# Four other byte offsets for the normed and the gated activations of a two-layer decoder trunk

## The chip, the cores and the metric

The kernel runs on one core of one Trainium2 chip. Times are device microseconds (us) of one execution, from its first to its last instruction on that core and with what the launch adds around them. A time is read as the median over runs.

## The reference

The program is a decoder trunk of two layers over 256 tokens of width 1024, all in float32. Each layer is: a SwiGLU feed forward, a token mixer, attention to a memory of 256 rows, and a second SwiGLU feed forward, each with an RMS norm before and after it.

```python
def swiglu(x, w_gate, w_up, w_down):
    return (jax.nn.silu(x @ w_gate) * (x @ w_up)) @ w_down
...
for l in range(DEPTH):                       # DEPTH = 2
    h = swiglu(rms_norm(x, ng[0]), ffn_w_gate[l, 0], ffn_w_up[l, 0], ffn_w_down[l, 0])
    x = x + 0.5 * rms_norm(h, ng[1])
    h = mixer(rms_norm(x, ng[2]))            # RWKV-7 and retention in layer 0,
    x = x + rms_norm(h, ng[3])               # sparse latent attention and a convolution in layer 1
    h = memory_xattn(rms_norm(x, ng[4]), mem_n, xa_wq[l], xa_wk[l], xa_wv[l], xa_wo[l])
    x = x + rms_norm(h, ng[5])
    h = swiglu(rms_norm(x, ng[6]), ffn_w_gate[l, 1], ffn_w_up[l, 1], ffn_w_down[l, 1])
    x = x + 0.5 * rms_norm(h, ng[7])
```

The four feed forwards are called (0, 0), (0, 1), (1, 0) and (1, 1) below: layer, and first or second of the layer. A weight of gate or up has 1024 rows and 2816 columns, one of down 2816 rows and 1024 columns.

## The kernel before, in words

**Products in parts.** Every float32 operand of the large products is split into two fp32r tiles, a high part (`whi`, `hhi`, `ahi`; a copy on ScalarE, L198, L241 and L251) and the rest (`wlo`, `hlo`, `alo`; a subtraction on VectorE, L199, L247 and L252). One product is then three matmuls (`mm3`, L255 to L258): high by high, high by low, low by high, added up in one PSUM bank. Each matmul has its own weight load on TensorE: an operand that is loaded (128x128, the *stationary* one) and an operand that streams through it column by column (the *moving* one).

**The tiles in question.** The normed activations of a feed forward, transposed, lie in a pair `hhi`, `hlo` that `new_h` allocates (L118): 8 blocks of 256 tokens side by side, one block for each 128 features. The gated activations, transposed too, lie in pairs `ahi`, `alo` (and `ahi0`, `alo0` for the first 512 features) that `products` allocates inside `ffn` (L483). In the built program each of these tiles begins on a multiple of 256 bytes in its partition. Each is allocated 64 elements (256 bytes) longer than its data, and the data begin 48 elements, that is 192 bytes, after the tile's beginning:

```python
return tuple(p.tile([P, DT * S + 64], F32R, name=name, bufs=1)[:, shift:shift + DT * S].rearrange(
    "p (k n) -> p k n", k=DT) for name in ("hhi", "hlo"))        # shift=48
...
return tuple(fp.tile([P, n * S + 64], F32R, name=part + name, bufs=bufs)[:, 48:48 + n * S].rearrange(
    "p (k n) -> p k n", k=n) for part in ("ahi", "alo"))
```

The weight tiles `whi` and `wlo` begin on a multiple of 256 bytes without an offset. The pairs that the mixers and the attention hand to their output projections (`new_h(keep, 0)`) have offset 0. The mixers' own input pair and the memory's pair have 192.

**A feed forward** (`ffn`, L478) first makes 512 columns of gate and up with the activations stationary (128 tokens at a time) and the weights moving: matmuls of 512 columns (L429, L434 in `project`, or L256 to L258 by `proj_nat`). Then come nine groups of 256 columns (`group_t`, `proj_t`): here a 128x128 block of the weight is stationary and the activations are moving, 256 columns (the 256 tokens) in each matmul, 48 for gate (`pg`) and 48 for up (`pu`) in a group. Behind each group the down projection of the features before it follows (`down`, tile `pd`): the gated activations are stationary and the weights of down are moving, 512 columns in each matmul.

**Order.** Inside the nine groups a scheduler sets the order by data and buffers; at the seams between stages (`bridge`, `lead_in`, `mix_in`, `start`) the order is written out by hand. All weights come by SP's DMA queue as float32 into `wst` and are split on ScalarE and VectorE beside the matmuls.

Of the kernel before, what the change touches and what calls it, by code (L numbers as in the profile page):

```python
# [11 lines left out]
F32R = mybir.dt.float32r  # L12
# [5 lines left out]
P = 128  # L18
S = 256
# [75 lines left out]
def tile_hybrid_trunk(ctx: ExitStack, tc: tile.TileContext, a: dict, out: bass.AP, stop=None):  # L95
# [13 lines left out]
    def bank(tag, name):  # L109
        return psum.tile([P, 512], F32, name=name, tag=tag)  # L110
# [3 lines left out]
    pv = keep.tile([P, 56], F32, name="pv")  # L114
    hneg = keep.tile([P, 4], F32, name="hneg")
    ones = keep.tile([P, 32], F32, name="ones")[:, 0:1]

    def new_h(p, shift=48):  # L118

        return tuple(p.tile([P, DT * S + 64], F32R, name=name, bufs=1)[:, shift:shift + DT * S].rearrange(  # L120
            "p (k n) -> p k n", k=DT) for name in ("hhi", "hlo"))
# [87 lines left out]
    def wunit(w, k0, kt, c0, n, only=None):  # L209
        return unit(*wload(w, k0, kt, c0, n), only)  # L210

    def nat(w, n=512):
        return [wload(w, 2 * i, 2, 0, n) for i in range(4)]
# [36 lines left out]
    def split(src, hi, lo):  # L250
        nc.scalar.activation(hi, src, AF.Copy)  # L251
        nc.vector.tensor_sub(lo, src, f32(hi))  # L252

    def mm3(ps, lh, rh, first, last):
        (l_hi, l_lo), (r_hi, r_lo) = lh, rh  # L255
        nc.tensor.matmul(ps, l_hi, r_hi, start=first, stop=False)  # L256
        nc.tensor.matmul(ps, l_hi, r_lo, start=False, stop=False)  # L257
        nc.tensor.matmul(ps, l_lo, r_hi, start=False, stop=last)  # L258


    def proj_nat(ps, h, t, units, kt):
        k = 0
        tot = len(units) * kt
        for hi, lo in units:
            for i in range(kt):
                s = slice(t * P, (t + 1) * P)
                mm3(ps, (h[0][:, k, s], h[1][:, k, s]), (hi[:, i, :], lo[:, i, :]), k == 0, k == tot - 1)
                k += 1
# [11 lines left out]
    def group_t(w, c0, h, name, us=None):  # L280
        us = us or [wunit(w, 4 * i, 4, c0, 256) for i in range(2)]
        ps = bank("pa", name)
        for f in range(2):
            proj_t(ps[:, f * S:(f + 1) * S], h, us, 4, f)
        return ps
# [132 lines left out]
    def in_order():  # L418
        return tc.manual_schedule(engines={ET.DVE, ET.Activation, ET.PE})
# [56 lines left out]
    def ffn(l, j, h, fp, lead, gpost, nxt, mid=None, follow=None):  # L476
        wg, wu, wd = a["ffn_w_gate"][l, j], a["ffn_w_up"][l, j], a["ffn_w_down"][l, j]
        pss = None  # L478
        kt_total = FF // P
        kt_at = 0  # L480

        ug, uu, done = lead
        def products(name, n, bufs):  # L483

            return tuple(fp.tile([P, n * S + 64], F32R, name=part + name, bufs=bufs)[:, 48:48 + n * S].rearrange(
                "p (k n) -> p k n", k=n) for part in ("ahi", "alo"))

        act = products("0", 4, 1)
        for t in range(2):
            if t < len(done):  # L490
                pg, pu = done[t]
            else:
                pg, pu = bank("pa", "pg"), bank("pa", "pu")
                proj_nat(pg, h, t, ug, 2)
                proj_nat(pu, h, t, uu, 2)
            sg = fp.tile([P, 512], F32, name="sg", bufs=2)
            nc.scalar.activation(sg, pg, AF.Silu)
            nc.vector.tensor_mul(sg, sg, pu)
            tr = bank("fr", "tra")
            for i in range(4):  # L500
                nc.tensor.transpose(tr[:, i * P:(i + 1) * P], sg[:, i * P:(i + 1) * P], ident)
            o = (slice(None), slice(None), slice(t * P, (t + 1) * P))
            split(tr.rearrange("p (k n) -> p k n", k=4), act[0][o], act[1][o])

        pss = [[bank(tag, "pd") for tag in ("iv", "bk")] for _ in range(2)]

        def down_unit(kt):
            return wunit(wd, kt, 1, 0, D)

        def down(act, i, kt, t, u, qs=(0, 1)):  # L510
            s = slice(t * P, (t + 1) * P)
            for q in qs:
                c = slice(q * 512, (q + 1) * 512)
                mm3(pss[t][q], (act[0][:, i, s], act[1][:, i, s]), (u[0][:, 0, c], u[1][:, 0, c]),
                    kt == 0, kt == kt_total - 1)

        todo = [(act, i, i) for i in range(4)]
        ngroups = (FF - 512) // 256
        for g in range(ngroups):
            if g > 1 and mid:  # L520
                next(mid, None)
            if g == 1:
                gpost = gpost()
            c0 = 512 + 256 * g
            pg = group_t(wg, c0, h, "pg")
            pu = group_t(wu, c0, h, "pu")
            sg = fp.tile([P, 512], F32, name="sg", bufs=2)
            nc.scalar.activation(sg, pg, AF.Silu)
            af = fp.tile([P, 512], F32, name="af", bufs=2)
            nc.vector.tensor_mul(af, sg, pu)  # L530
            act = products("", 2, 2)
            fl = lambda z: z.rearrange("p k n -> p (k n)")
            split(af, fl(act[0]), fl(act[1]))
            if g < ngroups - 1:
                for (ac, i, kt) in todo:
                    u = down_unit(kt)
                    for t in range(2):
                        down(ac, i, kt, t, u)
                todo = []
            todo += [(act, i, 4 + 2 * g + i) for i in range(2)]  # L540
        if follow:
            gn, hn, loads, only = follow
            ahead = units_ahead([(*wload(wd, kt, 1, 0, D), only) for (_, _, kt) in todo] + loads)
            ahead.load(3)
            us = ahead.take(4)
            po = [post(pss[t], gpost, t, True) for t in range(2)]
            no = [rms(env["x"][:, t, :], gn, hn, t) for t in range(2)]

            def tp(t, q):

                order = {(0, 0): ((0, 0), (0, 1), (1, 0), (1, 1), (0, 2), (0, 3)), (0, 1): ((1, 2), (1, 3))}
                for c, i in order.get((t, q), [(q, i) for i in range(4)]):
                    down(*todo[i], t, us[i], (c,))

            with in_order():
                bridge(tp, po, no, ahead, 3 if only is None else 3)
                return nxt(po[1], no[1], hn, ahead)

        us = [down_unit(kt) for (_, _, kt) in todo]
        for t in range(2):  # L560
            for q in range(2):
                for e, u in zip(todo, us):
                    down(*e, t, u, (q,))
            post(pss[t], gpost, t, True).all()
            nxt(t)
# [38 lines left out]
    def cross(l, sp, y, w_unit, w_out, kts):  # L604
# [1 line left out]
        wq, wo = a["xa_wq"][l], a["xa_wo"][l]  # L606
        wg, wu = a["ffn_w_gate"][l, 1], a["ffn_w_up"][l, 1]
        sc = 128.0 ** -0.5
        h, h2 = new_h(sp), new_h(sp)
        cx = ExitStack()  # L610
        xp = cx.enter_context(tc.tile_pool(reuse_waits="tile", name=f"xa{l}", bufs=1))
        gp, gn = ng(l, 3), ng(l, 4)
# [33 lines left out]
        o = new_h(keep, 0)  # L646
# [953 lines left out]

    with stage("0", None, None, 4) as sp:
        env["x"] = sp.tile([P, 2, D], F32, name="x", bufs=1)
        h = new_h(sp)
        hm, _ = ffn_mix(0, sp, h, keep, start(h), early())
        mem_k(0, mh, memp)
    for l in range(depth):
        if l % 2 == 0:
            y, w_unit = even_mixer(l, hm, mh if l == 0 else None, mem_scope if l == 0 else None)
            kts = [0, 1, 2, 3, 4, 5, 6, 7]
        else:  # L1610
            y, w_unit = odd_mixer(l, hm, pss)
            hm_scope.close()
            kts = [4, 5, 6, 7, 0, 1, 2, 3]
        if l == 0:
            xpool = pool("x", side="right", reuse_waits="tile")
        with stage(f"x{l}", [xd[t] for t in range(2)] if l == 0 else None, xpool) as sp:
            h2, lead = cross(l, sp, y, w_unit, a["od_w_out" if l % 2 else "ev_w_out"][l // 2], kts)
            with tc.tile_pool(reuse_waits="tile", name=f"ffb{l}", bufs=1) as fp:
                if l + 1 < depth:
                    h3 = new_h(sp)  # L1620
                    lead = ffn(l, 1, h2, fp, lead, lambda: ng(l, 7), lead_in,
                               follow=(ng(l + 1, 0), h3, nat(a["ffn_w_gate"][l + 1, 0]) + nat(a["ffn_w_up"][l + 1, 0]), None))
                else:
                    ffn(l, 1, h2, fp, lead, lambda: ng(l, 7), finish)
            if l + 1 < depth:
                hm_scope = ExitStack()
                hm, pss = ffn_mix(l + 1, sp, h3, hm_scope.enter_context(
                    tc.tile_pool(name=f"hm{l + 1}", bufs=1, side="right", reuse_waits="tile")), lead)
# [45 lines left out]
```

## Time and profile before

| | |
|---|---|
| median of 2 runs | 1194.47 us (1193.23 to 1195.7) |
| the profiled execution's own time | 1193.1 us |
| its span in the trace | 1191.2 us |
| TensorE busy with matmuls | 1139.0 us (96%), 7956 matmuls |
| TensorE busy with weight loads | 1006.0 us (84%) |
| VectorE, ScalarE, GpSimd busy | 727.9, 608.5, 69.9 us |
| DMA, mean over the span | 180 GB/s |

A matmul's duration in the trace overlaps that of the next one, since matmuls are pipelined. What a matmul takes of the time is read from the distance between its start and the next one's start: two rows of the timeline and the number of matmuls between them give it. In the rows below, names such as `pu<-hhi,whi` read: the PSUM tile that is written, then the moving operand, then the stationary one.

### The profile page before, as it was taken

What the parts mean: (1) busy time and instruction counts of PE and PEld (TensorE: products, weight loads), DVE (VectorE), ACT (ScalarE), POOL (GpSimd) and SP (SyncE); (2) the same over time, 40 slices, a digit from 0 to 9 for tenths busy, and PEclk for the clock granted to TensorE, in tenths of its full rate; (3) what the DMA queues carried; (4) which work ended last, traced back from release to release, by engine and by line L of the source; (5) the groups of instructions that cost most, each with busy time, mean ns of one, the idle gap of its engine ahead of it and who ended that gap; (6) DMA issues with size and microseconds to landing.
All of it is one profiled execution on the core that took longest, in us unless ns stands there. A gap on an engine that the chain in (4) does not pass through costs nothing.

```text
span 1191.2 us, 19770 instructions
## 1 busy us (share of the span) xinstructions
PE 1139.0 (96%) x7956; PEld 1006.0 (84%) x7956; DVE 727.9 (61%) x1097; ACT 608.5 (51%) x908; POOL 69.9 (6%) x104
## 2 busy tenths in 40 slices
PE   6999999999998989999999999999899999999997
PEld 5899999997776767799999789999788777899996
DVE  5645555587567587755554755454669588654552
ACT  5545445754334567644443654444456467544441
POOL 0000000012241010000000000000100000000000
PEclk9999999999999999999999999999999999999999
DMA  6877665643652775476665476665433664676650
GB/s 217 247 256 227 206 182 173 195 154 102 170 158 77 217 270 157 157 220 193 199 192 176 135 237 209 196 186 166 140 89 89 224 218 124 212 214 205 188 171 36
DMA packets 152267, 213.99 MB, mean 180 GB/s; under 512 B 21872, under 2 KB 115184, under 8 KB 152176
## 3 DMA queue, kind: packets, MB, share of 16 engines
q1 hardware_dynamic: 138224, 206.58, 56.5%
q10 hardware_dynamic: 13216, 3.54, 1.3%
q0 software_dynamic: 736, 2.62, 0.7%
q8 instruction: 62, 1.02, 0.3%
q14 instruction: 29, 0.24, 0.1%
HBM read 206.67 MB, written 6.05 MB: 179 GB/s over the span
## 4 chain that ended last, share of the span: by engine, by line
PE 71%; DVE 12%; ACT 5%; DMA 5%; issue 3%; POOL 2%; ACTq 0%; SPq 0%; POOLq 0%; DVEq 0%
PE pd L258 6%; PE pd L257 6%; PE pd L256 6%; PE pg L258 6%; PE pg L257 6%; PE pg L256 6%; PE pu L257 6%; PE pu L256 6%; PE pu L258 6%; DVE wlo L199 2%; DVE wlo L247 2%; POOL rstd L304 1%; ACT whi L198 1%; PE trh L353 1%; ACT sq L326 1%
## 5 line engine op out<-in xcount | busy, mean ns | idle before, releaser
L199 DVE TENSOR_TENSOR wlo<-wst,whi 128x1024 fp32r<-128x1024 f32 x290 | 356.0, 1229 | 307.7 <-ACT whi L198 303.2
L198 ACT ACTIVATE whi<-wst 128x1024 fp32r<-128x1024 f32 x290 | 306.9, 1060 | 329.7 <-PE pg L257 66.5
L257 PE MATMUL pg<-hlo,whi 128*128 128x256 f32 x576 | 160.2, 278 | 0.0
L256 PE MATMUL pg<-hhi,whi 128*128 128x256 f32 x576 | 160.2, 278 | 0.0
L258 PE MATMUL pg<-hhi,wlo 128*128 128x256 f32 x576 | 160.0, 278 | 0.0
L258 PE MATMUL pu<-hhi,wlo 128*128 128x256 f32 x576 | 159.2, 276 | 0.0
L256 PE MATMUL pu<-hhi,whi 128*128 128x256 f32 x576 | 159.1, 276 | 0.0
L257 PE MATMUL pu<-hlo,whi 128*128 128x256 f32 x576 | 159.1, 276 | 0.0
L258 PE MATMUL pd<-whi,alo 128*128 128x512 f32 x352 | 138.6, 394 | 0.0
L257 PE MATMUL pd<-wlo,ahi 128*128 128x512 f32 x352 | 137.8, 393 | 0.0
L256 PE MATMUL pd<-whi,ahi 128*128 128x512 f32 x352 | 137.2, 390 | 0.0
L257 PEld LDWEIGHTS pg<-hlo,whi 128*128 128x128 f32 x576 | 108.9, 189 | 1.4
L256 PEld LDWEIGHTS pg<-hhi,whi 128*128 128x128 f32 x576 | 108.6, 188 | 1.4
L258 PEld LDWEIGHTS pg<-hhi,wlo 128*128 128x128 f32 x576 | 108.7, 189 | 0.0
L247 DVE TENSOR_TENSOR wlo<-wst,whi 128x1024 fp32r<-128x1024 f32 (+1 forms) x68 | 81.8, 1215 | 43.5 <-ACT whi L241 42.5
L257 PEld LDWEIGHTS pu<-hlo,whi 128*128 128x128 f32 x576 | 108.3, 188 | 0.0
L258 PEld LDWEIGHTS pu<-hhi,wlo 128*128 128x128 f32 x576 | 108.1, 188 | 0.0
L256 PEld LDWEIGHTS pu<-hhi,whi 128*128 128x128 f32 x576 | 108.1, 188 | 0.0
L241 ACT ACTIVATE whi<-wst 128x1024 fp32r<-128x1024 f32 (+1 forms) x68 | 70.3, 1052 | 36.0 <-PE pu L257 9.1
L304 POOL TENSOR_TENSOR rstd<-s,hneg 128x1 f32<-128x1 f32 x34 | 23.9, 703 | 943.9 <-DVE s L374 943.9
L258 PEld LDWEIGHTS pd<-whi,alo 128*128 128x128 f32 x352 | 66.2, 188 | 14.1 <-DVE alo L252 0.6
L256 PEld LDWEIGHTS pd<-whi,ahi 128*128 128x128 f32 x352 | 66.1, 188 | 13.8 <-ACT ahi L251 0.7
(374 smaller groups left out, 2010.5 us busy)
## 6 DMA issues: line engine op xcount, KB each, us to landing
wst<-in_ffn_w_gate_dram SPq DMA_DIRECT2D x88, 512.0 KB, 4.5
wst<-in_ffn_w_up_dram SPq DMA_DIRECT2D x88, 512.0 KB, 4.3
wst<-in_ffn_w_down_dram SPq DMA_DIRECT2D x88, 512.0 KB, 4.4
wst<-in_ev_w_in_dram SPq DMA_DIRECT2D x30, 512.0 KB, 3.9
gb<-in_norm_g_dram SPq DMA_DIRECT2D x16, 512.0 KB, 5.9
wst<-in_od_w_in_dram SPq DMA_DIRECT2D x12, 512.0 KB, 4.2
wst<-in_xa_wk_dram SPq DMA_DIRECT2D x8, 512.0 KB, 4.4
wst<-in_xa_wv_dram SPq DMA_DIRECT2D x8, 512.0 KB, 4.3
```

Of the source, the lines that this page charges most:

```text
L198: nc.scalar.activation(hi[:, :m], st[:, :m], AF.Copy)
L199: env["split"] = nc.vector.tensor_sub(lo[:, :m], st[:, :m], f32(hi[:, :m])).ins
L241: nc.scalar.activation(hi[:, :kt * n], st[:, :kt * n], AF.Copy)
L247: env["split"] = nc.vector.tensor_sub(lo[:, :m], st[:, :m], f32(hi[:, :m])).ins
L256: nc.tensor.matmul(ps, l_hi, r_hi, start=first, stop=False)
L257: nc.tensor.matmul(ps, l_hi, r_lo, start=False, stop=False)
L258: nc.tensor.matmul(ps, l_lo, r_hi, start=False, stop=last)
L304: nc.gpsimd.tensor_tensor(dst, src, hneg[:, :n], op=ALU.pow)
L326: nc.scalar.activation(sq, self.src[:, q * 512:(q + 1) * 512], AF.Square, scale=1.0 / math.sqrt(D), accum_out=self.ss[:, q:q + 1])
L353: nc.tensor.transpose(tr[:, i * P:(i + 1) * P], self.xg[q][:, i * P:(i + 1) * P], ident)
```

## The change

Nothing but byte offsets changes. A table gives each feed forward its own offset, in elements of 4 bytes: 52, 44, 56 and 40, which is 208, 176, 224 and 160 bytes, for (0, 0), (0, 1), (1, 0) and (1, 1). `products` takes it for the gated activations, and the four calls of `new_h` that make a feed forward's normed activations take it too. All tiles keep their places and their sizes; on each of the five engines the same instructions stand in the same order, with the same waits. In one feed forward these operands move: the moving operand of 864 matmuls of 256 columns (9 groups of 96), the stationary operand of 96 matmuls of 512 columns for gate and up and of 264 for down, and the places that ScalarE and VectorE write (15 splits each). In four feed forwards that makes 3456, 384 and 1056 matmuls. The mixers, the memory's keys and values, and the attention's output projection keep their offsets.

```diff
+    OFF_LINES = {(0, 0): 52, (0, 1): 44, (1, 0): 56, (1, 1): 40}
...
         def products(name, n, bufs):
 
-            return tuple(fp.tile([P, n * S + 64], F32R, name=part + name, bufs=bufs)[:, 48:48 + n * S].rearrange(
+            o = OFF_LINES[l, j]
+            return tuple(fp.tile([P, n * S + 64], F32R, name=part + name, bufs=bufs)[:, o:o + n * S].rearrange(
                 "p (k n) -> p k n", k=n) for part in ("ahi", "alo"))
...
-        h, h2 = new_h(sp), new_h(sp)
+        h, h2 = new_h(sp), new_h(sp, OFF_LINES[l, 1])
...
-        h = new_h(sp)
+        h = new_h(sp, OFF_LINES[0, 0])
...
-                    h3 = new_h(sp)
+                    h3 = new_h(sp, OFF_LINES[l + 1, 0])
```

## Rows read from the trace of the kernel before

**Rows 1.** The page: span, busy time, granted clock by slice, chain by engine.
```profile
span 1191.2 us, 19770 instructions
...
PE 1139.0 (96%) x7956; PEld 1006.0 (84%) x7956; DVE 727.9 (61%) x1097; ACT 608.5 (51%) x908; POOL 69.9 (6%) x104
...
PEclk9999999999999999999999999999999999999999
...
PE 71%; DVE 12%; ACT 5%; DMA 5%; issue 3%; POOL 2%; ACTq 0%; SPq 0%; POOLq 0%; DVEq 0%
```

**Rows 2.** Windows: the four feed forwards' groups; window: length, busy by engine, clock, DMA.
```profile
42.60:203.00 160.40, 160.40 (x1137) 149.13 (x1137) 89.85 (x94) 79.54 (x101) 2.03 (x3) 1.00 0.70 215
502.30:662.00 159.70, 159.02 (x1132) 148.03 (x1132) 84.31 (x84) 73.04 (x85) 1.16 (x2) 1.00 0.64 191
688.70:851.00 162.30, 160.32 (x1133) 148.40 (x1132) 84.75 (x87) 74.48 (x87) 1.48 (x2) 1.00 0.63 189
1024.30:1184.00 159.70, 159.08 (x1132) 147.75 (x1131) 79.86 (x79) 67.67 (x77) 0.55 (x1) 1.00 0.57 175
```

**Rows 3.** Costliest groups by form: line, tiles, shapes, count | busy us, mean ns.
```profile
L257 PE MATMUL pg<-hlo,whi 128*128 128x256 f32 x576 | 160.2, 278 | 0.0
...
L258 PE MATMUL pd<-whi,alo 128*128 128x512 f32 x352 | 138.6, 394 | 0.0
...
L429 PE MATMUL pg<-whi,hhi 128*128 128x512 f32 x40 | 16.5, 413 | 0.5 <-ACT hhi L251 0.5
...
L256 PE MATMUL pu<-whi,hhi 128*128 128x512 f32 x24 | 9.3, 388 | 0.0
```

**Rows 4.** Timeline of TensorE, second group of (0, 0): start us, duration us, instruction.
```profile
70.48 0.28 PE L256 MATMUL pu<-hhi,whi 128*128 128x256 f32 x1
...
75.92 0.39 PE L256 MATMUL pd<-whi,ahi 128*128 128x512 f32 x1
```

**Rows 5.** Timeline of TensorE, first group of (0, 0).
```profile
48.17 0.28 PE L256 MATMUL pu<-hhi,whi 128*128 128x256 f32 x1
...
53.82 0.40 PE L256 MATMUL pd<-whi,ahi 128*128 128x512 f32 x1
```

**Rows 6.** Timeline of TensorE at half clock, before that group.
```profile
42.78 0.41 PE L256 MATMUL pg<-hhi,whi 128*128 128x256 f32 x1
...
43.42 0.41 PE L256 MATMUL pg<-hhi,whi 128*128 128x256 f32 x1
```

**Rows 7.** Timeline of TensorE behind down projections, and an output projection's two ends.
```profile
65.02 0.28 PE L256 MATMUL pg<-hhi,whi 128*128 128x256 f32 x1
65.14 0.29 PE L257 MATMUL pg<-hlo,whi 128*128 128x256 f32 x1
65.27 0.28 PE L258 MATMUL pg<-hhi,wlo 128*128 128x256 f32 x1
65.39 0.28 PE L256 MATMUL pg<-hhi,whi 128*128 128x256 f32 x1
...
81.42 0.28 PE L256 MATMUL pg<-hhi,whi 128*128 128x256 f32 x1
...
936.90 0.39 PE L256 MATMUL po<-whi,hhi 128*128 128x512 f32 x1
...
947.78 0.39 PE L256 MATMUL po<-whi,hhi 128*128 128x512 f32 x1
```

**Rows 8.** Timeline of TensorE in the mixer of layer 1, matmuls of 456 columns.
```profile
852.76 0.37 PE L429 MATMUL pdi<-wlo,hhi 128*128 128x456 f32 x1
852.97 0.37 PE L429 MATMUL pdi<-whi,hhi 128*128 128x456 f32 x1
...
856.68 0.99 PE L434 MATMUL pdi<-whi,hlo 128*128 128x456 f32 x4
```

**Rows 9.** Splits on L252 and L251 by tile: ns min/median/max, first and last start.
```profile
L252 DVE TENSOR_TENSOR alo<-af,ahi x36: 683/686/693, 55.8 to 1175.0; 128x512 fp32r<-128x512 f32 x36
...
L252 DVE TENSOR_TENSOR hlo<-yc,hhi x2: 685/686/686, 933.9 to 939.6; 128x512 fp32r<-128x512 f32 x2
...
L251 ACT ACTIVATE ahi<-af x36: 614/632/636, 54.7 to 1174.3; 128x512 fp32r<-128x512 f32 x36
...
L251 ACT ACTIVATE hhi<-yc x2: 633/634/635, 932.9 to 938.6; 128x512 fp32r<-128x512 f32 x2
```

## The prediction, made before the changed kernel had run

> **What bounds the kernel now.** I read the page first. TensorE is busy with matmuls for 1139.0 of 1191.2 us, the clock is granted in full in all 40 slices, and the chain that ends last runs over TensorE for 71% [rows 1]. Then the windows of the four feed forwards: in each, matmuls fill all but 2 us of some 160 us, while VectorE and ScalarE are busy for about half of it and the DMA engines for 0.57 to 0.70 [rows 2]. So the distance between the starts of two matmuls is the price of everything here, and the change touches just the operands of these matmuls: 3456 of 256 columns (two products of three matmuls, 576 each), 1056 of 512 columns for down (three of 352) and 384 of 512 columns for gate and up (six groups of 40, six of 24) [rows 3].
>
> The timeline gives the distances. The reader is to see that one and the same form has two levels. In the second group of (0, 0), 48 matmuls of 256 columns take 75.92 - 70.48 = 5.44 us, 113.3 ns each [rows 4]. In the first group 48 of the same form, on the same activations with the same 192 bytes, take 53.82 - 48.17 = 5.65 us, 117.7 ns each [rows 5]. For 512 columns: from 53.82 to 65.02 there are 48 for down, 233.3 ns each [rows 5, 7]; from 75.92 to 81.42 there are 24, 229.2 ns each [rows 4, 7]; and in the output projection, where the stationary operand lies on a 256-byte line, 48 from 936.90 to 947.78 take 226.7 ns each [rows 7]. The switch is seen at 65.02: the first three distances of the next group are 0.12, 0.13 and 0.12 us, and from 65.39 to 70.48 the other 45 take 113.1 ns each [rows 7, 4]. Order, waits and clock are alike on both sides, so the level is a matter of how the reads of the moving operand and of the next weight load fall against each other. An offset can change that.
>
> At half clock (1.2 GHz) the same matmul took (43.42 - 42.78) / 3 = 213 ns [rows 6]; half of that is 106.7 ns for 256 columns at 2.4 GHz. The lower level is 6.6 ns above it, so at full clock something beside the columns is paid for, in proportion to the bytes: 226.7 for 512 columns is twice 113.3 [rows 4, 7]. Cut into 64-byte stretches (16 columns), 256 columns are 16 of them, 7.08 ns each, of which 6.67 are the columns and 0.41 is the rest. 192 bytes are three such stretches; none of 208, 176, 224 and 160 is a whole number of them, so 1024 bytes of data touch 17 stretches where they touched 16. That is the whole change for a moving operand.
>
> **The change part by part.**
>
> *Instructions.* None is added, removed or moved, on no engine and in no DMA queue, so no wait changes its place: 0 us.
>
> *Moving operand, 3456 matmuls.* The price of the 17th stretch has no row of its own. Its lower bound is the 0.41 ns for one more edge: 3456 x 0.41 = 1.4 us. Its upper bound is a whole stretch although only part of it is used: 3456 x 7.08 = 24.5 us. The nearest row is the mixer's projection, whose moving operand has 456 columns (28.5 stretches) and begins on a 256-byte line in one matmul and 32 bytes after one in the next. Touched are 29 stretches either way. Whole stretches would make 29 x 7.08 = 205.4 ns, used bytes 28.5 x 7.08 = 201.9 ns; 19 matmuls from 852.76 to 856.68 took 206.3 ns each [rows 8]. What the 512-column matmuls with a stationary operand at 192 bytes pay over 226.7 ns is 2.5 ns at the lower level and 6.6 ns at the upper. By used bytes the mixer pays 4.4 ns, between these two; by whole stretches 0.9 ns, below both. The row is nearer to used bytes, and I take +1.4 us. An offset of 32 bytes is not paid twice over in any case, which speaks for 224 and 160; for 208 and 176, which are 16 bytes off, no row speaks.
>
> [...]
>
> *Stationary operand, 1440 matmuls of 512 columns.* The weight load runs beside the matmul before it, so only its effect on that matmul's reads counts. The rows give 226.7 ns at offset 0 and 229.2 or 233.3 at 192 [rows 4, 5, 7]. Bounds: 1440 x (226.7 - 229.2) = -3.6 us and 1440 x 4.1 = +5.9 us. All four offsets are nearer to 192 than to 0 or 256, so I take 0 here apart from the level.
>
> *The level.* A feed forward that stays on the upper level pays 864 x 4.4 + 264 x 4.1 = 4.9 us. Before, only first groups do [rows 5, 7]. Bounds: none, 0, and all, 3456 x 4.4 + 1440 x 4.1 = 21 us. I take half of one feed forward, 2.5 us: the lower level was found again at a seam without any help [rows 7], and a shift of 16 or 32 bytes is small, but four offsets give four occasions to lose it.
>
> [...]
>
> *Splits.* 60 on ScalarE and 60 on VectorE write to the new places. Those of SBUF input write to 192 bytes in 632 and 686 ns and to offset 0 in 634 and 686 ns [rows 9]; the difference of at most 2 ns makes 0.1 us, and they lie beside matmuls. Were that cover gone (the last split before a down projection), it would still be 0.1 us: 0.
>
> *Sum.* +1.4 + 0 + 2.5 + 0 = +3.9 us. The profiled execution's own time is 1193.1 us, span 1191.2; with the sum 1197.0. It lies 1.4 us below the median of the runs shown, 1194.5, so against the median the forecast is **1198 us**.
>
> **The rivals.**
>
> *A. A stretch that is touched is paid whole.* Place: the 3456 matmuls of the nine groups. Price 7.08 ns, +24.5 us, 1219 us. It decides as soon as the 17th stretch costs a full one; 2% is 23.9 us, so this rival lies on the edge, a little beyond it, and one feed forward on the upper level as well makes 1224. For it: the surplus over the columns goes with the bytes, as if the supply were the limit, and then a partly used fetch has the price of a full one. Against it: the mixer's 206.3 ns leave only 0.9 ns for the weight load's part [rows 8].
>
> *B. All four fall to the upper level and stay.* +21 us, 1215 us. For it: the upper level held from 48.17 for 17 us, through 48 matmuls for up and 48 for down [rows 5, 7]. Against it: the lower level held everywhere behind the seam.
>
> *C. The new offsets suit the weight loads better.* The 512-column matmuls go to 226.7 ns, -3.6 us, and the levels stay: 1191 us. For it: 192 is not the cheapest offset for a stationary operand, 0 is [rows 7]. Against it: four different offsets would all have to be better ones.
>
> *D. The offsets are free.* All terms are 0: 1194.5 us. For it: in the mixer, starts 32 bytes apart cost alike [rows 8]. Against it: the two levels and the 226.7 ns show that the two streams of reads do meet [rows 4, 5, 7]. It would come out the same if the change did not do what it says, that is, if the tiles began elsewhere than on multiples of 256 bytes; the built program has them there, before and after. [...]
>
> **How the numbers follow.** Forecast (the prices stay between the two levels, some of the 17th stretch is paid) 0.33, its own range 1196 to 1206, from the first term alone to two feed forwards on the upper level. A 0.25, B 0.13, C 0.11, D 0.15. The last 0.03 is for a larger price of the two offsets that are 16 bytes off a 32-byte step, for which no row gives a bound. The range must leave out at most 2 in 10: it goes from C less the spread of 1.2 us, 1190, to 1222, which cuts off a third of A and the last 0.03. A difference of 2% is about what a measurement of this kernel can tell from no change. Slower by over 2% (above 1218.4): 0.6 of A, 0.15 of B and the last 0.03, together 0.20. Faster by over 2%: no term reaches -24 us, 0.01. Within 2%: 0.79.
>
> **What the profile of the changed kernel would show.** The 256-column matmuls of each feed forward's groups: 113.7 ns apart for the forecast, 113.3 for D, 120 for A, 117.7 for B, and each offset may answer for itself. Down's: 229 for the forecast and for D, 227 for C, 233 for B. The mixers' 256-column matmuls, which keep 192, stay at their two levels. Splits stay at 632 and 686 ns. VectorE, ScalarE and the DMA share of the windows stay; if instead TensorE shows idle time inside the groups, some supply of weights has become the bound, and the prediction is wrong in a way that no term covers. It is also wrong if any of the four offsets shows a distance outside 113 to 121 ns.

## The result and the profile after

The changed kernel takes 1209.92 us (median of 2 runs, 1209.54 to 1210.3) against 1194.47: a ratio of 1.0144, 95% interval 1.0121 to 1.0167, +15.4 us. That lies inside the range of 1190 to 1222, and outside the forecast's own 1196 to 1206. Its profiled execution takes 1209.54 us, span 1207.7, which is 16.5 us over the span before.

Page of the changed kernel: span, busy time, granted clock, chain by engine, and two of the costliest groups (busy us, mean ns of one). Its lines stand 3 (inside `ffn` 4) lower in the code than those of before.
```profile
span 1207.7 us, 19770 instructions
...
PE 1159.8 (96%) x7956; PEld 1021.3 (85%) x7956; DVE 728.4 (60%) x1097; ACT 609.4 (50%) x908; POOL 69.8 (6%) x104
...
PEclk9999999999999999999999999999999999999999
...
PE 71%; DVE 12%; DMA 6%; ACT 5%; issue 3%; POOL 2%; SPq 0%; ACTq 0%; POOLq 0%; DVEq 0%
...
L260 PE MATMUL pg<-hlo,whi 128*128 128x256 f32 x576 | 162.4, 282 | 0.0
...
L261 PE MATMUL pd<-whi,alo 128*128 128x512 f32 x352 | 138.7, 394 | 0.0
```
Beside [rows 1] TensorE's busy time has grown by 20.8 us for matmuls and by 15.3 for weight loads, which run beside them. Counts, clock, VectorE and ScalarE are as before, and the chain's shares within a point. The mean duration of a matmul of the groups goes from 278 to 282 ns [rows 3], but durations overlap; the price is in the windows and in the starts.

Windows of the changed kernel over the same matmuls as [rows 2]: window, length, busy by engine (PE, PEld, DVE, ACT, POOL), clock, DMA.
```profile
40.60:204.70 164.10, 164.10 (x1138) 152.28 (x1137) 90.85 (x96) 80.59 (x101) 2.03 (x3) 1.00 0.69 213
505.70:670.90 165.20, 164.22 (x1133) 152.84 (x1132) 84.35 (x84) 73.64 (x86) 1.18 (x2) 1.00 0.63 185
697.70:864.20 166.50, 164.92 (x1134) 151.99 (x1132) 84.18 (x86) 74.58 (x87) 1.48 (x2) 1.00 0.61 183
1036.60:1200.50 163.90, 163.46 (x1132) 151.08 (x1131) 79.78 (x79) 67.74 (x77) 0.56 (x1) 1.00 0.57 170
```
The four are 3.7, 5.5, 4.2 and 4.2 us longer, 17.6 together, still without a new gap in TensorE's work. So everything lies in the feed forwards, and in how far apart matmuls start.

Timeline of TensorE in the changed kernel, a group of each feed forward: up's first matmul, down's first, the next gate's first. Columns: start us, duration us.
```profile
68.33 0.28 PE L259 MATMUL pu<-hhi,whi 128*128 128x256 f32 x1
...
74.05 0.39 PE L259 MATMUL pd<-whi,ahi 128*128 128x512 f32 x1
...
79.60 0.28 PE L259 MATMUL pg<-hhi,whi 128*128 128x256 f32 x1
...
535.64 0.28 PE L259 MATMUL pu<-hhi,whi 128*128 128x256 f32 x1
...
541.37 0.40 PE L259 MATMUL pd<-whi,ahi 128*128 128x512 f32 x1
...
727.69 0.28 PE L259 MATMUL pu<-hhi,whi 128*128 128x256 f32 x1
...
733.37 0.39 PE L259 MATMUL pd<-whi,ahi 128*128 128x512 f32 x1
...
1066.03 0.28 PE L259 MATMUL pu<-hhi,whi 128*128 128x256 f32 x1
...
1071.65 0.39 PE L259 MATMUL pd<-whi,ahi 128*128 128x512 f32 x1
```
Up's 48 matmuls take 119.2 ns each at 208 bytes (5.72 us), 119.4 at 176, 118.3 at 224 and 117.1 at 160, where [rows 4] have 113.3. Down's 24 behind the first take 231.3 ns each (79.60 - 74.05). The mean of all distances between starts in a feed forward (taken from the whole trace, here and below) says the same:

| | (0, 0) | (0, 1) | (1, 0) | (1, 1) |
|---|---|---|---|---|
| offset, bytes | 208 | 176 | 224 | 160 |
| 256 columns before, ns | 113.97 | 113.62 | 114.02 | 113.61 |
| 256 columns after | 118.35 | 119.29 | 118.36 | 117.48 |
| down before | 229.83 | 228.90 | 229.74 | 229.10 |
| down after | 232.08 | 230.05 | 233.25 | 233.16 |

The differences of the four feed forwards, added up, are 18.3 ns for the first pair of lines and 11.0 for the second. The first pair makes 864 x 18.3 ns = 15.8 us, the second 264 x 11.0 = 2.9, and the 512-column gate and up (229.2 before, 230.1 to 233.7 after) some 1.3: 20.0 us. The span shows 16.5. The other 3.5 us are given back outside the change's operands, and the trace shows where only in part. The second group starts at 62.61 in place of 65.02 us [rows 7] though its matmuls are dearer: weights of up had landed at 36.16 us, where they landed at 37.07 before, and a stretch at half clock that the kernel before has at 40.3 to 43.8 us [rows 6] (granted clock 0.51 there) is missing after (1.00). Two such stretches later, from 313.7 and 443.4 us on (0.50 up to 317.0, 0.53 up to 447.0, and 1.00 before in both), are new and take part of it back. The mixers' matmuls, untouched, stand oftener on their lower level (input projections 115.05 before, 113.94 ns after, in the mean).

Splits after, by tile: ns min/median/max, first and last start.
```profile
L255 DVE TENSOR_TENSOR alo<-af,ahi x36: 683/685/693, 54.5 to 1191.3; 128x512 fp32r<-128x512 f32 x36
...
L254 ACT ACTIVATE ahi<-af x36: 612/633/635, 53.4 to 1190.6; 128x512 fp32r<-128x512 f32 x36
```
To four other offsets they write as fast as to 192 [rows 9].

### The profile page after: what moved, and what is told of

Same layout as the page of the kernel before. It is cut to its first block, busy times and chain, and to the rows that moved or that the text cites. A ratio compares the mean times of both kernels' runs of the same rounds, so it can differ in the third digit from the quotient of the medians.

```text
span 1207.7 us, 19770 instructions
## 1 busy us (share of the span) xinstructions
PE 1159.8 (96%) x7956; PEld 1021.3 (85%) x7956; DVE 728.4 (60%) x1097; ACT 609.4 (50%) x908; POOL 69.8 (6%) x104
## 4 chain that ended last, share of the span: by engine, by line
PE 71%; DVE 12%; DMA 6%; ACT 5%; issue 3%; POOL 2%; SPq 0%; ACTq 0%; POOLq 0%; DVEq 0%
PE pd L259 6%; PE pd L261 6%; PE pd L260 6%; PE pg L261 6%; PE pg L260 6%; PE pu L260 6%; PE pg L259 6%; PE pu L259 6%; PE pu L261 6%; DVE wlo L202 2%; DVE wlo L250 2%; ACT whi L201 1%; PE trh L356 1%; POOL rstd L307 1%; DMA wst<-in_ffn_w_down_dram 1%
## 5 line engine op out<-in xcount | busy, mean ns | idle before, releaser
L260 PE MATMUL pu<-hlo,whi 128*128 128x256 f32 x576 | 162.2, 282 | 0.0
L259 PE MATMUL pu<-hhi,whi 128*128 128x256 f32 x576 | 161.8, 281 | 0.0
L261 PE MATMUL pu<-hhi,wlo 128*128 128x256 f32 x576 | 161.7, 281 | 0.0
L250 DVE TENSOR_TENSOR wlo<-wst,whi 128x1024 fp32r<-128x1024 f32 (+1 forms) x68 | 81.8, 1215 | 43.9 <-ACT whi L244 43.3
```

What stands on the lines that cost most here:

```text
L250: env["split"] = nc.vector.tensor_sub(lo[:, :m], st[:, :m], f32(hi[:, :m])).ins
```

## The experiments

The theories. **S**: whole and part 64-byte stretches of the moving operand decide, as the prediction had it. **R**: the distance, modulo 256 bytes, between the places of the moving and the stationary operand decides. **P**: the offset of down's stationary operand decides, through the phase in which it leaves the groups behind it. Below, `OFF_LINES` holds the normed activations' offsets and `OFF_ACT` the gated ones', in elements of 4 bytes; wherever `OFF_ACT` stands, `products` reads it as in the first experiment. The time of the kernel before is that of the same series of runs, so it differs a little from one experiment to another.

### The normed half alone
```diff
+    OFF_ACT = {(0, 0): 48, (0, 1): 48, (1, 0): 48, (1, 1): 48}
...
-            o = OFF_LINES[l, j]
+            o = OFF_ACT[l, j]
```


> The normed activations keep 208, 176, 224 and 160 bytes, the gated ones are back at 192. Theory S (stretches: a moving operand that does not start on a 64-byte boundary pays for one more 64-byte stretch): the 256-column matmuls stay at 118.4, 119.3, 118.4 and 117.5 ns as in the changed kernel, down's fall back to 229; of the 15.4 us some 13 stay, 1207 us. Theory R (what counts is how the moving and the stationary operand lie to each other): the same for the 256 columns, since neither of their operands moves back, and 229 for down. Rival P (the down projection leaves TensorE in the phase that puts the next group on the upper level, so the gated offsets are the cause): the 256-column matmuls fall to 113.8 and the time to 1196 us.

Measured: 1209.23 us against 1194.43, ratio 1.0126 (1.0091 to 1.0161). The 256-column matmuls stand at 119.2, 119.2, 118.4 and 118.7 ns, down back at 229.2 in the mean of the four. The normed half alone carries nearly the whole loss; P as the cause falls. By the distances the groups alone lost 17.5 us (864 times the four differences to the kernel before), 1.7 more than in the change. So the gated offsets do act on the groups of the change, and as a gain: behind downs at 192, normed activations at 208 cost 119.2 ns in all groups, behind downs at 208 every third group costs less. Up's first matmul and down's in the third group of (0, 0), in the changed kernel and then with the normed half alone:
```profile
85.20 0.28 PE L259 MATMUL pu<-hhi,whi 128*128 128x256 f32 x1
...
90.80 0.40 PE L259 MATMUL pd<-whi,ahi 128*128 128x512 f32 x1
```
```profile
85.20 0.28 PE L260 MATMUL pu<-hhi,whi 128*128 128x256 f32 x1
...
90.92 0.39 PE L260 MATMUL pd<-whi,ahi 128*128 128x512 f32 x1
```
That is 116.7 and 119.2 ns. At 160 it is 117.4 behind the downs of the change and 118.7 behind downs at 192.

### Whole stretches
```diff
+    OFF_LINES = {(0, 0): 0, (0, 1): 16, (1, 0): 32, (1, 1): 48}
+    OFF_ACT = {(0, 0): 32, (0, 1): 48, (1, 0): 0, (1, 1): 16}
```


> Normed activations at 0, 64, 128 and 192 bytes, gated ones at 128, 192, 0 and 64, all multiples of 64. Theory S: 113.3 to 113.8 ns for 256 columns in all four feed forwards, down at 226.7 to 229 in all four, so 1191 to 1195 us. Theory R: the four distances to the stationary weights (0, 64, 128, 192 bytes) give four prices of 256 columns, some of them at 117.7 or above, and down's four prices differ too (226.7 for 0, 229 for 192, others up to 233), 1195 to 1205 us.

Measured: 1208.34 us, ratio 1.0125 (1.0095 to 1.0155). (0, 0), with its normed activations on a 256-byte line, up's first matmul and down's:
```profile
69.46 0.28 PE L260 MATMUL pu<-hhi,whi 128*128 128x256 f32 x1
...
75.22 0.39 PE L260 MATMUL pd<-whi,ahi 128*128 128x512 f32 x1
```
5.76 us for 48, 120.0 ns each, with exactly 16 stretches touched: dearer than any of the four offsets of the change. In the mean 0, 64 and 128 cost 119.9, 117.8 and 119.8 ns. S has fallen, and rival A with it. At 192, in (1, 1), groups now alternate between 117.8 and 113.4 ns (115.9), with gated activations at 64 ahead of them.

### Finer offsets, and a scan
```diff
+    OFF_LINES = {(0, 0): 49, (0, 1): 50, (1, 0): 24, (1, 1): 8}
+    OFF_ACT = {(0, 0): 4, (0, 1): 8, (1, 0): 12, (1, 1): 52}
```


> Normed activations at 196, 200, 96 and 32 bytes (4, 8, 32 and 32 past a 64-byte boundary), gated ones at 16, 32, 48 and 208. Theory S: every one of the four pays the same for 256 columns, 117.5 to 120.4 ns, 4 bytes past as much as 32 past. [...] Down (stationary operand off by 16, 32, 48, 16): 230 to 233.3 ns by what 208, 176, 224 and 160 showed.

Measured: 1215.16 us (one run). 196 bytes, 4 behind the cheap place, cost 121.7 ns:
```profile
69.16 0.29 PE L260 MATMUL pu<-hhi,whi 128*128 128x256 f32 x1
...
75.00 0.40 PE L260 MATMUL pd<-whi,ahi 128*128 128x512 f32 x1
```
The others: 200 bytes 120.1, 96 bytes 120.0, 32 bytes 116.7. Down at 16, 32, 48 and 208 bytes: 232.9 to 233.4.
```diff
+    OFF_LINES = {(0, 0): 4, (0, 1): 20, (1, 0): 36, (1, 1): 46}
+    OFF_ACT = {(0, 0): 20, (0, 1): 28, (1, 0): 60, (1, 1): 36}
```


> Normed activations at 16, 80, 144 and 184 bytes, gated ones at 80, 112, 240 and 144. Theory R: only the distance modulo 256 between the moving and the stationary operand counts, and 192 is one narrow cheap place: 184 (8 bytes below) costs 118 to 121 ns, since 196 (4 above) cost 121.7; 80 and 144 cost 117 to 120, 16 about 118. Rival R2 (the cheap place is a band between 176 and 196): 184 costs 114 to 116. Down: 230 to 234 ns at all four of 80, 112, 240 and 144, as at every offset tried but 0 and 192. Whole: 1208 to 1216 us.

Measured: 1210.18 us (one run). Normed at 16, 80, 144 and 184: 116.7, 118.3, 118.3 and 120.0 ns. For 184, up's first matmul and down's:
```profile
1064.71 0.28 PE L260 MATMUL pu<-hhi,whi 128*128 128x256 f32 x1
...
1070.48 0.39 PE L260 MATMUL pd<-whi,ahi 128*128 128x512 f32 x1
```
So 192 is a narrow place: 8 bytes below and 4 above cost 7 to 8 ns more. R2's band is not there. But it is not the only cheap place. Means hide levels: at 16 most groups stand at 116.6 or 118.8 ns, and two of (0, 0) at 113.4, the first one and one behind transposes of another stage, whose up and down start here:
```profile
118.48 0.28 PE L260 MATMUL pu<-hhi,whi 128*128 128x256 f32 x1
...
123.93 0.39 PE L260 MATMUL pd<-whi,ahi 128*128 128x512 f32 x1
```
Down at 240 was cheaper than expected, 227.9; at 80, 112 and 144 it took 231.9 to 233.2.

### Another place for the weights
```diff
-        hi = wp.tile([P, 1024], F32R, name="whi")
-        lo = wp.tile([P, 1024], F32R, name="wlo")
+        hi = wp.tile([P, 1024 + 16], F32R, name="whi")[:, 4:4 + 1024]
+        lo = wp.tile([P, 1024 + 16], F32R, name="wlo")[:, 4:4 + 1024]
```
(with normed activations at 208, 192, 16 and 0, gated ones at 0 in layer 0 and 16 in layer 1)

> All split weight tiles start 16 bytes past a 64-byte boundary (each is 64 bytes longer, so that their places within 256 bytes differ). Normed activations at 208, 192, 16 and 0 bytes; gated ones on 64-byte boundaries in (0, 0) and (0, 1), 16 past one in (1, 0) and (1, 1). Theory S: the 256 columns cost 118 to 120 ns in (0, 0) and (1, 0), whose moving operand is off, and 113.3 to 114 in (0, 1) and (1, 1), whose moving operand is on a boundary though the stationary one is off; down, whose moving operand is now off everywhere, pays 4 to 7 ns more than 229 in all four. Theory R: (0, 0) and (1, 0), where both operands are off by the same 16 bytes, fall to 113.3, and (0, 1) and (1, 1) rise to 118 to 120; down is at 229 in (1, 0) and (1, 1) and over it in (0, 0) and (0, 1).

Measured: 1209.96 us (one run). Each weight tile now begins 16, 80, 144 or 208 bytes after a 256-byte line, so every feed forward mixes four distances, with means of 117.3 to 118.5 ns: what S and R said of whole feed forwards cannot be read from them. Sorted by distance, stretches of equal ones give 113.3 to 114.3 ns at 192, though both operands lie off a line there (16 and 80, or 208 and 16), 119.6 at 128, 119.2 at 112, 117.8 to 118.3 at 0. That speaks for R at 192. At 0 it is some 2 ns less than whole feed forwards cost there, so the stretches, which are short, do not give every price. The next experiment asks it in the whole kernel; its activation tiles also lose their spare 256 bytes, which nothing needs at offset 0.
```diff
-    OFF_LINES = {(0, 0): 52, (0, 1): 44, (1, 0): 56, (1, 1): 40}
+    OFF_LINES = {(0, 0): 0, (0, 1): 0, (1, 0): 0, (1, 1): 0}
-    def new_h(p, shift=48):
+    def new_h(p, shift=0):
...
+        if id(wp) not in gaps:
+            gaps[id(wp)] = (wp, wp.tile([P, 16], F32R, name="gap", bufs=1))
         hi = wp.tile([P, 1024], F32R, name="whi")
         lo = wp.tile([P, 1024], F32R, name="wlo")
+        if len(gaps[id(wp)]) == 2:
+            gaps[id(wp)] += (wp.tile([P, 48], F32R, name="gap2", bufs=1),)
```


> Normed and gated activations at 0 in all four feed forwards and in the mixers, and all split weights 64 bytes behind a multiple of 256: every distance between moving and stationary operand is again that of the kernel before (normed less weight 192, weight less gated 64), though every single place is another. Only the attention's output projections change theirs (64 in place of 0, 288 matmuls). Theory R (the distance modulo 256 sets the price): 256-column matmuls at 113.3 to 114.2 ns with the upper level 117.8 in some first groups, down 229 to 229.8, output projection 229 to 233 in place of 228: 1194 to 1196 us, the time of the kernel before within 0.2%. Rival A (the place of the moving operand itself counts, as normed at 0 with the weights on 0 cost 119.9): 119.9 ns, 3456 x 6.1 = 21 us more, about 1213.

Measured: 1194.0 us against 1192.33, ratio 1.0015 (0.9994 to 1.0035). A group of (0, 1), up, down and the next gate:
```profile
533.48 0.28 PE L265 MATMUL pu<-hhi,whi 128*128 128x256 f32 x1
...
538.91 0.39 PE L265 MATMUL pd<-whi,ahi 128*128 128x512 f32 x1
...
544.41 0.28 PE L265 MATMUL pg<-hhi,whi 128*128 128x256 f32 x1
```
113.1 ns and 229.2 ns, the numbers of [rows 4, 7]. The same normed activations at 0 cost 120.0 with weights at 0 and 113.3 with weights at 64. The upper level, 117.8, stood longer than before only in (0, 0), through five groups, 115.89 instead of 113.97 in the mean: 864 x 1.9 = 1.7 us, as much as the difference of the medians. **R is shown for the distance of 192**: moved together by 64 bytes, the operands cost what they did before, and the place of the moving one by itself does not decide. For the other distances no pair was moved together through a whole kernel.

### Half a weight load
```diff
-    def proj_t(ps, h, units, kt, f):
+    def proj_t(ps, h, units, kt, f, m=P):
...
-                mm3(ps, (hi[:, i, s], lo[:, i, s]), (h[0][:, k, :], h[1][:, k, :]), k == 0, k == tot - 1)
+                c = slice(f * P, f * P + (P if k in (0, tot - 1) else m))
+                mm3(ps[:P if k in (0, tot - 1) else m], (hi[:, i, c], lo[:, i, c]), (h[0][:, k, :], h[1][:, k, :]), k == 0, k == tot - 1)
...
-            proj_t(ps[:, f * S:(f + 1) * S], h, us, 4, f)
+            proj_t(ps[:, f * S:(f + 1) * S], h, us, 4, f, 64 if name in ("pg", "pu") else P)
```
(with normed activations at 192, 208, 176 and 0, gated ones at 192)

> Normed activations at 192, 208, 176 and 0 bytes in (0, 0), (0, 1), (1, 0) and (1, 1), gated ones at 192 everywhere. In the nine groups of each feed forward, 36 of the 48 matmuls of a tile (all but the first and the last of the eight 128-row blocks) load 64 of the 128 stationary columns and so write 64 of 128 PSUM partitions; part of the products is left out, so only distances count. Theory R (what a 256-column matmul takes beyond its columns is paid to the next weight load, whose reads meet the moving operand's reads, the distance of the two places deciding how often): with half as many columns to load the surplus over 106.7 ns shrinks, in the mean of a group from 12.6 to about 8 ns at 208 and 176 (115 ns instead of 119.2) and from 13.2 to about 8 at 0 (115 instead of 119.9), and the offsets come closer together; 192 falls from 113.3 to 112 or so. Rival M (the price is the moving operand's own, the weight load only sits beside it): all four keep 113.3 (or 117.7), 119.2, 119.2 and 119.9 ns. [...]

Measured: 1197.87 us (one run, part of the products left out). (1, 1), normed at 0, 48 matmuls of up, 36 of them with 64 columns loaded:
```profile
1056.63 0.28 PE L260 MATMUL pu<-hhi,whi 128*128 128x256 f32 x1
...
1062.17 0.39 PE L260 MATMUL pd<-whi,ahi 128*128 128x512 f32 x1
```
115.4 ns each instead of 120.0. Where a matmul and the next both load 64 columns, the mean is 113.9 at 0, 116.9 at 208 and 115.8 at 176; where both load 128, 119.7, 119.8 and 118.9. So the price depends on how many columns are loaded, and M falls as it was put. What is not separated: a matmul with half the columns loaded also writes half the PSUM partitions. And the price goes with a matmul's own load rather than with the next one's: at 0, a matmul on 128 columns with 64 for the next still costs 118.3 ns, one on 64 with 128 for the next 113.5. So it is not shown which reads meet. There is no fall at 192: 115.4 and 115.1 (both levels mixed), where R expected a fall to 112. Over the 106.7 ns that [rows 6] give as an estimate for the columns, 8.7 and 8.4 ns remain there.

### The gated half alone, and gated activations at 0
```diff
-    OFF_LINES = {(0, 0): 52, (0, 1): 44, (1, 0): 56, (1, 1): 40}
+    OFF_LINES = {(0, 0): 48, (0, 1): 48, (1, 0): 48, (1, 1): 48}
+    OFF_ACT = {(0, 0): 52, (0, 1): 44, (1, 0): 56, (1, 1): 40}
```


> The gated activations' part of the change alone: 208, 176, 224 and 160, the normed ones back at 192. Theory R: the 256-column matmuls stay at 113.3 to 113.8 ns (117.7 where a first group takes the upper level); down takes 232.1, 230.0, 233.3 and 233.2 ns as in the changed kernel, 264 x (2.7 + 0.6 + 3.9 + 3.8) = 2.9 us more: 1197.4 us. Together with the normed part alone (+14.8) that would make 17.7, some 2 us more than the whole change showed. Rival P (down's phase decides for the groups behind it): the 256-column matmuls go to 117.5 to 119 and the time to 1210.

Measured: 1200.59 us against 1192.34, ratio 1.0075 (1.0059 to 1.0091), +8.2: neither 3 nor 16. Down cost what it should, 231.8, 230.1, 233.3 and 233.2 ns. But the groups, at 192 as before, went to 115.82, 115.44, 117.76 and 114.07. (0, 0), from up of the second group to up of the fourth:
```profile
69.27 0.28 PE L260 MATMUL pu<-hhi,whi 128*128 128x256 f32 x1
...
74.92 0.40 PE L260 MATMUL pd<-whi,ahi 128*128 128x512 f32 x1
...
80.49 0.28 PE L260 MATMUL pg<-hhi,whi 128*128 128x256 f32 x1
...
85.93 0.28 PE L260 MATMUL pu<-hhi,whi 128*128 128x256 f32 x1
...
91.37 0.39 PE L260 MATMUL pd<-whi,ahi 128*128 128x512 f32 x1
...
96.93 0.28 PE L260 MATMUL pg<-hhi,whi 128*128 128x256 f32 x1
...
102.58 0.28 PE L260 MATMUL pu<-hhi,whi 128*128 128x256 f32 x1
```
117.7 ns in the first stretch, then a down, then 113.3 (5.44 us for gate, 5.44 for up), then a down, then 117.7 (5.65). From there on each down of 24 matmuls at 208 turns the level over, and at 176 too (the first down, of 48, does so at 176 and not at 208); at 224 the upper one stays for good; at 160 the lower one does, from the second group on. The sum, 7.9 ns x 864 = 6.8 us for the groups (the four surpluses added up) and 2.9 for down, makes 9.7, somewhat over what was measured. P is right about this where the normed activations are at 192; in the change, where they are not, its part is the gain of 1.7 us above.

From here to gated activations at 0, the normed ones staying at 192:
```diff
-    OFF_ACT = {(0, 0): 52, (0, 1): 44, (1, 0): 56, (1, 1): 40}
+    OFF_ACT = {(0, 0): 0, (0, 1): 0, (1, 0): 0, (1, 1): 0}
```


> Normed activations at 192 as in the kernel before, gated ones at 0. Theory R: down goes from 229.4 to 226.7 ns per matmul, since moving and stationary operand then both lie on a 256-byte line as in the attention's output projection: 1056 x 2.7 = 2.8 us less, 1191.6 us against 1194.4. The 256-column matmuls keep 113.3 to 113.8, if the level that a group takes does not depend on the down projection ahead of it. Rival P (down's phase sets the level of the group behind it): groups that follow go to 117.7, 32 of 36 groups x 96 x 4.4 = 13.5 us more less 2.8, about 1205.

Measured: 1201.69 us against 1192.34, ratio 1.0079 (1.0064 to 1.0095). (0, 1), up, down and the next gate; then (0, 0) at the group behind eight small transposes of another stage:
```profile
533.11 0.28 PE L260 MATMUL pu<-hhi,whi 128*128 128x256 f32 x1
...
538.76 0.39 PE L260 MATMUL pd<-whi,ahi 128*128 128x512 f32 x1
...
544.20 0.28 PE L260 MATMUL pg<-hhi,whi 128*128 128x256 f32 x1
```
```profile
112.92 1.04 PE L357 MATMUL trh<-ident,xn 128*128 128x128 f32 x8
113.72 0.37 PE L260 MATMUL pg<-hhi,whi 128*128 128x256 f32 x1
...
119.25 0.28 PE L260 MATMUL pu<-hhi,whi 128*128 128x256 f32 x1
...
124.69 0.39 PE L260 MATMUL pd<-whi,ahi 128*128 128x512 f32 x1
```
Down took 226.7 (5.44 us for 24), as hoped, 2.6 us less in the kernel. And 32 of 36 groups took 117.8 ns: 864 x 14.0 ns over the four = 12.1 us more. Behind the transposes the same form takes 113.3 (119.25 to 124.69). 9.5 us by these two terms, 9.4 measured. The rival's arithmetic held, R's did not.

### What carries the level
Both blocks of a group's gated activations need not lie alike. With `n` = 2 the first was put at 0 and the second at 192, then the other way round (normed activations at 192; the first 512 features, `n` = 4, stay at 192):
```diff
...
+            if n == 2:
+                zs = [t[:, 0:n * S + 64] for t in ts]
+                return tuple(bass.AP(tensor=z.tensor, offset=z.offset + 0, ap=[z.ap[0], [304, 2], [1, S]]) for z in zs)
...
```


> Normed activations at 192. Of the two 128-feature blocks of a group's gated activations the first lies at 0, the second at 192, so the down projection behind a group does 12 matmuls with a stationary operand at 0 and then 12 at 192. Theory L (with normed at 192 a group has two levels, 113.3 and 117.8 ns, and the last matmuls of the down projection ahead of it choose): groups stay at 113.3 as in the kernel before, down takes 226.7 in its first half and 229 in its second, 432 x 2.5 = 1.1 us less: 1191 to 1194 us, 0.1% below the kernel before. Rival M (the gated offset as a whole decides, or a mixture does it): 117.8 ns behind most seams, 10 us more.

> The same with the blocks the other way round: the first at 192, the second at 0, so the last 12 matmuls ahead of each group are at 0. Theory L: 117.8 ns in all groups but the first of a feed forward, as where both blocks are at 0: 3456 x 3.6 = 12 us more, 1.1 less, about 1203. Rival M: the same as with the other order of blocks.

Measured: 1201.38 us, ratio 1.0085 (1.0053 to 1.0117), and 1205.3 (one run). (0, 1) of the first of the two: up of the second group, down, gate and up of the third:
```profile
532.93 0.28 PE L259 MATMUL pu<-hhi,whi 128*128 128x256 f32 x1
...
538.37 0.39 PE L259 MATMUL pd<-whi,ahi 128*128 128x512 f32 x1
...
543.85 0.28 PE L259 MATMUL pg<-hhi,whi 128*128 128x256 f32 x1
...
549.50 0.28 PE L259 MATMUL pu<-hhi,whi 128*128 128x256 f32 x1
```
113.3 before a down that ends with twelve matmuls at 192, and 117.7 behind it. L has fallen: the last matmuls do not choose. Both orders lose the lower level at the first down with mixed blocks; the twelve at 0 are enough. The last experiment asks for a version that beats both kernels, with normed activations at 192:
```diff
+    OFF_ACT = {(0, 0): 60, (0, 1): 60, (1, 0): 60, (1, 1): 60}
```


> Normed activations at 192, gated ones at 240 in all four feed forwards: the one offset, beside 192, at which down was cheap without every matmul taking the same 226.7 ns (227.9 in the mean). Theory L2 (the level, 113.3 or 117.8 ns, is carried along from matmul to matmul; down's own pattern of distances carries the lower level over or loses it; 192 carries it over, 0, 176, 208 and 224 lose it, 160 carries it over): if 240 carries it over, groups at 113.3 to 113.9 and 1056 x 1.5 = 1.6 us less, about 1190.8; if it loses it, 117.8 in most groups, 12 us more less 1.6, about 1203. The trace so far does not say which. Rival (the price of down alone counts): 1190.8 in any case.

Measured: 1201.53 us against 1190.6, ratio 1.0096 (1.008 to 1.0112). Down 227.5 to 227.9 ns; the groups 116.4 to 117.4. 240 loses the level too. With normed activations at 192, gated ones at 0, 64, 176, 208 and 240 lose it at least at times, behind 224 it was never there, 160 and 192 keep it, and 192 is the cheaper of the two (229.4 against 233.2). No version found beats the kernel before.

## Why the prediction came out as it did

The range held; the forecast was 11.9 us too low against the median, with a change of +15.4 us where +3.9 was summed up. That the range held is owed to its width, which made room for the rivals A and B; neither of them came about, so this was luck and not the mechanism. Step by step:

- **What bounds** and **instructions**: right. Start distances moved, and TensorE had no new gap. Of the signs that would have made the prediction wrong none showed: the means of the four offsets lie between 117 and 120 ns, inside 113 to 121.
- **Splits**: right, 0.
- **Moving operand**: the step that failed. It made the surplus a matter of 64-byte stretches touched and took 1.4 us. The 64-byte stretch had no row of its own, and whole stretches (0, 64 and 128: 119.9, 117.8 and 119.8 ns) turned out as dear as broken ones (117.5 to 119.3), so there is no 17th stretch to be paid for; the term belongs to the distance to the weights and measured 15.8 us together with the level. The 0.41 ns in it rest on an estimate: the trace grants a clock of 0.50 over 42.70 to 43.50 us, where 256 columns in 213 ns [rows 6] are 1.2 a ns, and 1.00 in the groups, for which 2.4 a ns and 106.7 ns are worked out by doubling; no run shows the columns by themselves. The term had bounds of 1.4 and 24.5, and the error was in choosing between them: the mixer's 456-column row [rows 8] was taken as the nearest because its moving operand starts in two places. Its stationary operand lies at 192, so its distances were 64 and 96, and the groups' 192 was not among them. A row is near only if both operands stand as in the case asked.
- **Stationary operand**: 0 taken, 4.2 measured (2.9 for down, 1.3 for gate and up), inside its bounds of -3.6 and 5.9. "Nearer to 192 than to 0 or 256" does not hold for 224, which lies midway between 192 and 256, and was no argument: nearness in bytes does not order the prices, as 196 against 192 shows for the other operand.
- **The level**: taken at 2.5 as a chance of half a feed forward. At the changed offsets the two levels of 113.3 and 117.8 do not occur. Two of the four have levels of their own (208: 116.7 and 119.2, 160: 117.4 and 118.7), and the changed downs chose lower ones there: 1.7 us less than with the normed half alone, not 2.5 more. With the normed activations at 192, the gated half alone cost 6.8 us by the level, more than was taken. The reading of [rows 4, 5] behind the term, that it matters how the two operands fall against each other, is borne out at 192 by moving both. It was used as a small extra term; it was the main one.
- **The rivals**: A gave too much (1219) by a mechanism that is refuted. B's number (1215) was the nearest from above, its mechanism half right: means of 117.5 to 119.3 instead of 117.7, but as prices of distances, not as a fall to the old upper level. C and D are refuted by down's 230 to 233 and by the groups' 118.

What a matmul takes while its load runs beside it goes with the place of the weights and with how much of them is loaded: with the weights 64 bytes on, the same normed activations went from 120.0 to 113.3 ns, and with half the columns loaded from 119.7 to 113.9. That it is the reads of the two operands that meet is the author's reading; no run here looks at the reads themselves.

The four offsets of the change are multiples of 16 bytes. The runs show no step between such multiples and other offsets: 0 and 128 cost 119.9 and 119.8 ns, 184 and 200, which are none, 120.0 and 120.1, and 196, none either, is the dearest at 121.7.

Left open: why the distance acts at all, why 192 holds 113.3 through whole feed forwards and 16 only in single groups, and what turns the level over. Shown is only that down's offset does it, that the level can change behind transposes (from 117.8 to 113.3 ns), and that a down's last twelve matmuls do not choose it (113.3 ahead of one that ends at 192, 117.7 behind it). A period of 128 bytes is out (96 and 224 cost 120.0 and 118.4 ns); that it is 256 and not longer follows from no run, since the tiles were laid out in multiples of 256.

## What to carry to other kernels

Where TensorE is the bound, look at where the moving and the stationary operand lie against each other and try offsets as a pair: moving one of them by 4 bytes cost 7% of a matmul here, moving both by 64 cost nothing that could be told from noise. Parts do not add up: the normed half alone cost 14.8 us, the gated half 8.2, both 15.4. By the distances, 6.8 us of the gated half are the upper level of normed activations at 192, which is not there once these have moved, and at their new places the gated offsets gave 1.7 us back. And a cheaper form can spoil the one behind it, as gated activations at 0 did: 2.6 us won in down, 12.1 lost in the groups.

## What the runs showed of the hardware that was not expected

- A 256-column fp32r matmul with a 128x128 weight load beside it, at full clock (1.00 in the windows of the groups before and after, 0.993 to 0.996 in the mean of every profiled run), takes, by the place of its moving operand less that of the weights, modulo 256, with every level seen: 192: 113.3 or 117.8; 16: 113.4, 116.6 or 118.8; 32: 116.7; 208: 116.7 or 119.2; 144: 116.7 or 118.7; 160: 117.4 or 118.7; 64: 117.8; 80: 118.3; 224: 118.4; 176: 119.3; 0: 119.9; 128: 118.6 or 120.0; 96 and 184: 120.0; 200: 120.1; 196: 121.7 ns. Only 192 was tried at a second place through whole feed forwards.
- One form with 512 columns takes 226.7 ns with both operands on a 256-byte line (228.5 behind groups at 128), 227.9 with the stationary one at 240, 229 at 192, 230 at 176, and 232 to 234 at most other offsets tried. Its price depends on more than the distance: at 16 bytes gate and up took 227.2 in one kernel, down 233.4 in another.
- The level of a form is carried through others of another form: in (0, 1) of the kernel before the lower one, 113.3 ns, stands in all nine groups, with downs at 192 (228.9 ns) between them; with gated activations at 0 the upper one, 117.8, stands in 32 of 36 groups, with downs at 226.7 between them.
